# The second matrix of a convolution branch: half of its columns by seven block products instead of eight, in a planned order

## The chip, the core and the metric

The kernel runs on one core of a Trainium2 chip. The engines that matter are TensorE (matrix products; PE in the profile, PEld its weight loads), VectorE (DVE), ScalarE (ACT), and the two queues that start transfers from main memory in this part, SyncE (SP) and GpSimd (POOL). Each engine works through its own list of instructions in order, and waits where an instruction needs something that another engine or a transfer hasn't finished. The metric is the time of one execution on the device, in microseconds (us).

## The reference

One layer of a decoder, 256 tokens and 16 learned ones ahead of them, width D = 2048, all in 32-bit floats:

```python
u = rms_norm(h, g_pre_mix)
proj = u @ w_in          # z_pool 1024 | v_conv 1024 | g_conv 1024 | gate_a 2048 | gate_b 2048
y_a = causal_multiscale_pool(z_pool, w_pool_grp, pool_scale) @ w_pool_out   # 1024 x 2048
a = v_conv * sigmoid(g_conv)
c = depthwise_causal_conv(a, w_dw, 31 taps) + b_dw
y_b = silu(layer_norm(c)) @ w_conv_out                                      # 1024 x 2048
m = sigmoid(gate_a) * y_a + sigmoid(gate_b) * y_b
h = h + rms_norm(m @ w_o)
h = h + rms_norm(square(relu(rms_norm(h) @ w_up)) @ w_down)
```

The change concerns the product with `w_conv_out`, 256 x 1024 times 1024 x 2048, and the work on `c` ahead of it.

## The kernel before

**Products in three terms.** Every factor is split in two parts of a shorter format, a high one (ScalarE casts) and a low one (VectorE subtracts the high part from the original), and a product is the sum of high x high, high x low and low x high. A weight tile is 512 rows by 512 columns (128 partitions x 2048 numbers, 1 MB). It is loaded into one of three rooms named `raw` (SP), cast into one of three `hi` slots and subtracted into one of three `lo` slots; `open_chunk` and `fetch` do that up to two tiles ahead of TensorE. A *block product* is one block of 128 tokens by 512 rows times one weight tile: 4 x 3 = 12 matmuls of 128 x 512 that add up in one bank of the accumulator memory. There are eight banks, six named `acc` and two `misc`.

**Stages.** First the columns of `v_conv` and `g_conv` in tiles of 256 columns (`project`), then `z_pool`, then the sixteen blocks of the two gates (`project_t`, tiles of 5.44 us, 32 of them), the pool's group map, its output matrix (`acc_po`, 8 tiles), the conv's output matrix (`acc_co`, 8 tiles), then W_o (`o_a`, `o_b`, `o_c`), and the two matrices of the feed-forward part. W_o and the feed-forward part already use seven block products for eight (Winograd's form of Strassen's scheme): sums of weight tiles, sums of token blocks, and results added to or subtracted from several outputs. Their order is written out by hand (`STEPS`) and the instructions of each engine are put in order by the class `Plan`: each piece of work has an engine, a cost and the names that it reads and writes; `order` derives from TensorE's sequence when each piece is due, and gives every engine, among the pieces that can start, the one due first. Pieces that no product of the same plan needs have no due time and go in the order in which they were added.

**Work between the products.** Ahead of the plans, vector work is put in a list `pending` with a cost for each item. After each half tile `drain` gives the list a credit, `fill`/2 us, and issues items as long as the credit covers them. What ScalarE must do behind such an item is put in `late` and let go by the next `fetch`, behind that tile's cast. An entry `FETCH` in the list holds the items behind it until `late` is empty.

The 31 taps of the convolution run there: for each of eight tiles of 128 channels (`conv_tile`) one activation and thirty items `c = a[shifted] * tap + c` on VectorE, one after the other. Then come the layer norm's sums. The four steps that end the norm (`ln_items`: normed, with sixteen activations on ScalarE behind it, then swish, low, high) are put at the head of the list when the pool's output matrix begins.

**The conv's output matrix** is plain: for each of four column blocks n two tiles of 512 rows; each tile serves the two blocks of tokens, so two block products per tile, sixteen in all. Behind a column block VectorE multiplies the bank by the gate and adds the pool's part (`evac_conv`, two instructions per block of tokens), and TensorE transposes the result into `m` (`feature_steps`) one column block later. The transposes of the last column block run in W_o's plan behind its first product (`m_last`). Meanwhile GpSimd loads two sums of W_o tiles (`early_sums`): two plain loads, then two that add to what is there.

## Time and profile before

| | us |
|---|---|
| time, median of 3 runs | 1183.82 (1183.77 to 1184.33) |
| the profiled execution, its own time | 1184.32 |
| its span, first to last instruction | 1182.6 |
| TensorE busy | 1172.7 |
| VectorE busy | 1027.6 |
| ScalarE busy | 679.6 |
| pool's output matrix on TensorE | 333.19 to 376.74 |
| conv's output matrix on TensorE | 376.74 to 422.99, four transposes within W_o's first products |

The matmuls overlap in their pipeline, so one lasts longer than the distance to the next; the times of a stage come from the chain of work, where the first number is the start, the second the length, then engine, output and line, and how many instructions. A row of a timeline has the start, the length, the engine, the line, the operation with output and inputs, and in brackets how long the engine was idle before it and what ended that.

### The profile page before, as it was taken

The numbers are of one execution on the slowest core, as the hardware profiler recorded it, in microseconds if no ns is written. First come the engines' busy times: TensorE is split into PE (matmuls) and PEld (weight loads), VectorE is DVE, ScalarE is ACT, GpSimd is POOL, SyncE is SP. The second block draws the span as 40 slices with busy tenths as digits, with TensorE's granted clock in tenths as the row PEclk, the third lists the DMA queues.
The fourth block names the chain that finished last, engine by engine and source line by source line (L and its number), as shares of the span: only waits on it lengthen the run. The fifth ranks groups of instructions, "written<-read, shape, count | busy, mean of one in ns | idle before, by whom it ended". The sixth has DMA issues, their size and how long they took to land.

```text
span 1182.6 us, 15774 instructions
## 1 busy us (share of the span) xinstructions
PE 1172.7 (99%) x6351; PEld 1018.9 (86%) x6351; DVE 1027.6 (87%) x1095; ACT 679.6 (57%) x690; POOL 45.0 (4%) x51
## 2 busy tenths in 40 slices
PE   9999999999999999999999999999999999999997
PEld 9999988888888888898888888888888888888886
DVE  6899978999766799987998988989989989889865
ACT  6533344444584465756566766666656667666642
POOL 1000000000000001000001001000000010010000
PEclk9999999999999999999999999999999999999998
DMA  8655565655647967859869898988998898998861
GB/s 295 214 178 179 182 204 184 196 195 184 208 143 268 265 215 221 290 168 317 248 213 249 228 288 220 269 269 226 281 293 215 267 279 229 282 241 239 303 214 72
DMA packets 177882, 272.91 MB, mean 231 GB/s; under 512 B 4657, under 2 KB 92913, under 8 KB 176912
## 3 DMA queue, kind: packets, MB, share of 16 engines
q1 hardware_dynamic: 160176, 235.88, 59.0%
q0 software_dynamic: 16736, 34.76, 16.2%
q10 hardware_dynamic: 896, 1.25, 0.3%
q8 instruction: 50, 0.82, 0.3%
q14 instruction: 24, 0.20, 0.1%
HBM read 267.68 MB, written 4.19 MB: 230 GB/s over the span
## 4 chain that ended last, share of the span: by engine, by line
PE 99%; DVE 0%; DVEq 0%; issue 0%; ACT 0%; ACTq 0%
PE bank_u L498 18%; PE acc_gate L802 15%; PE bank_a L1787 10%; PE bank_u L504 9%; PE acc_up L1787 8%; PE bank_b L1787 7%; PE o_c L1170 6%; PE acc_z L493 4%; PE acc_co L802 4%; PE acc_po L802 4%; PE acc_v L493 3%; PE acc_g L493 3%; PE acc_vg L493 2%; PE acc_up L498 1%; PE bank_u L1787 1%; PE o_b L1170 1%
## 5 line engine op out<-in xcount | busy, mean ns | idle before, releaser
L498 PE MATMUL bank_u<-m,hi 128*128 128x512 f32 x960 | 329.4, 390 | 0.0
L504 PE MATMUL bank_u<-m,lo 128*128 128x256 f32 x960 | 265.5, 277 | 0.0
L276 ACT CAST hi<-raw 128x2048 fp32r<-128x2048 f32 (+2 forms) x94 | 151.0, 1620 | 188.1 <-PE acc_gate L802 64.0
L498 PEld LDWEIGHTS bank_u<-m,hi 128*128 128x128 f32 x960 | 180.2, 188 | 37.9
L279 DVE TENSOR_TENSOR lo<-raw,hi 128x2048 fp32r<-128x2048 f32 (+2 forms) x94 | 180.0, 1925 | 34.6 <-ACT hi L276 34.1
L1570 DVE TENSOR_TENSOR lo<-raw_m,hi 128x2048 fp32r<-128x2048 f32 x70 | 160.3, 2290 | 31.6 <-ACT hi L1566 31.5
L504 PEld LDWEIGHTS bank_u<-m,lo 128*128 128x128 f32 x960 | 180.3, 188 | 1.4
L1566 ACT CAST hi<-raw_m 128x2048 fp32r<-128x2048 f32 x70 | 133.9, 1912 | 73.7 <-DVE raw_m L1583 21.3
L802 PE MATMUL acc_gate<-hi,u_um 128*128 128x512 f32 x416 | 131.1, 389 | 0.0
L559 DVE SCALAR_TENSOR_TENSOR c<-a,taps,c 128x256 f32<-128x256 f32 x240 | 115.7, 484 | 6.8
L1787 PE MATMUL bank_a<-hi,forms 128*128 128x512 f32 (+1 forms) x288 | 93.5, 386 | 0.0
L802 PEld LDWEIGHTS acc_gate<-hi,u_um 128*128 128x128 f32 x416 | 78.1, 188 | 16.1
L802 PE MATMUL acc_gate<-lo,u_um 128*128 128x512 f32 x208 | 80.9, 389 | 0.0
L1570 DVE TENSOR_TENSOR lo<-raw_a,hi 128x2048 fp32r<-128x2048 f32 x29 | 66.4, 2290 | 10.8 <-ACT hi L1566 10.7
L1566 ACT CAST hi<-raw_a 128x2048 fp32r<-128x2048 f32 x29 | 55.4, 1910 | 35.4 <-PE bank_u L498 13.2
L1566 ACT CAST hi<-raw_c 128x2048 fp32r<-128x2048 f32 x27 | 51.5, 1909 | 27.2 <-PE bank_u L498 12.4
L1570 DVE TENSOR_TENSOR lo<-raw_c,hi 128x2048 fp32r<-128x2048 f32 x27 | 61.8, 2289 | 5.7 <-ACT hi L1566 5.6
L1787 PEld LDWEIGHTS bank_a<-hi,forms 128*128 128x128 f32 x288 | 53.9, 188 | 11.0
L1570 DVE TENSOR_TENSOR fourth_pair<-raw_m,fourth_pair 128x2048 fp32r<-128x2048 f32 x26 | 59.5, 2288 | 4.4 <-ACT fourth_pair L1566 4.4
L1650 ACT COPY half<-bank_u 128x256 f32<-128x256 f32 x60 | 22.2, 370 | 66.0 <-PE bank_u L504 66.0
L1787 PE MATMUL acc_up<-hi,forms 128*128 128x512 f32 x176 | 57.4, 390 | 0.0
L1787 PE MATMUL bank_a<-lo,forms 128*128 128x512 f32 (+1 forms) x144 | 55.6, 386 | 0.0
(419 smaller groups left out, 2265.0 us busy)
## 6 DMA issues: line engine op xcount, KB each, us to landing
raw<-in_w_in_dram SPq DMA_DIRECT2D x52, 1024.0 KB, 5.1
raw_m<-in_w_down_dram SPq DMA_DIRECT2D x38, 1024.0 KB, 7.0
raw_m<-in_w_down_dram POOLq DMA_DIRECT2D x22, 1024.0 KB, 10.6
raw_a<-in_w_up_dram SPq DMA_DIRECT2D x20, 1024.0 KB, 6.4
raw_c<-in_w_up_dram SPq DMA_DIRECT2D x19, 1024.0 KB, 6.9
raw_m<-in_w_up_dram SPq DMA_DIRECT2D x19, 1024.0 KB, 6.9
raw_a<-in_w_down_dram SPq DMA_DIRECT2D x13, 1024.0 KB, 7.3
raw_c<-in_w_down_dram SPq DMA_DIRECT2D x13, 1024.0 KB, 7.3
```

The costliest lines, as they stand in the source:

```text
L276: nc.scalar.copy(hi[:, sl, cs], raw[:, sl, cs])
L279: nc.vector.tensor_sub(lo[:, sl, cs], raw[:, sl, cs], f32(hi[:, sl, cs]))
L493: nc.tensor.matmul(acc, w[:, k[0], cs], act[:, k[1], a, off:], start=first and n == 0, stop=last and n == 2)
L498: nc.tensor.matmul(acc.rearrange("p (a t) -> p a t", a=2)[:, :, ts], hi[:, k[0], cs], act[:, k[1], :, off + ts.start:off + ts.stop], start ...
L504: nc.tensor.matmul(acc[:, :T], lo[:, k[0], cs], act[:, k[1], 0, off:], start=False, stop=stop, skip_group_check=True)
L559: nc.vector.scalar_tensor_tensor(c, conv["a"][:, q, i:i + T], taps[:, q, i:i + 1], c, op0=ALU.mult, op1=ALU.add)
L802: nc.tensor.matmul(acc, act(kk)[:, a_, ts_], w_[:, k, :], start=kk == 0 and n == 0, stop=kk == nk - 1 and n == 2)
L1170: nc.tensor.matmul(acc, form(k, a_), box[w_][:, k, :], start=start and k == 0 and n == 0, stop=stop and k == CK - 1 and n == 2, skip_group ...
L1566: nc.scalar.copy(box["hi"], raw)
L1570: nc.vector.tensor_sub(box["lo"], raw, f32(box["hi"]))
L1650: nc.scalar.copy(box[j], accs[j][:, :T])
L1787: nc.tensor.matmul(acc, forms[h][:, f, k, a_, :], box[w_][:, k, cs], start=start and k == 0 and n == 0, stop=stop and k == KH - 1 and n == ...
```

## The change

The first two column blocks of the conv's output matrix (n = 0 and 1) are computed by seven block products instead of eight, the last two as before. The sequence on TensorE is written out in `ORDER`: units 1 to 7 are the seven products, X20a is column block 2, upper 512 rows, first block of tokens, and so on, f00 is the transposes of column block 0, first tokens. A new plan, `cplan`, orders the stage.

- Products 1, 6, 7 and 4 add up in one bank (`ch`); ScalarE copies what stands there after 1, 6 and 7 (`keep`). 2 has a bank of its own, 5 and 3 share one. VectorE joins copies and banks (`joined`) and applies the gates.
- Three weight tiles are sums of two, two and four tiles. They lie in the room of the gates' input `u` (`conv_wide`, tag `um`), and GpSimd loads them when the gates are done: three plain loads and five that add. Tile 6 is first used as tile 5, and then tile 3 is added to it on VectorE.
- The token blocks' sums (`conv_sums`) and four of their forms (`conv_high`, `conv_low`) are new work of VectorE and ScalarE.
- The two sums of W_o tiles are loaded behind product 3 instead of at the start of the stage.
- The taps of two channel tiles are put into the list alternately (`conv_pair`), the credits rise from 2.4 and 2.5 to 3.0 and 2.9, and the first two steps of the norm move into the gates' stage.
- In the first two column blocks a tile's two parts serve one product; the X tiles still serve two.
- W_o's plan expects VectorE free 3.0 us after its start instead of 2.2.

```diff
-    for w, nk in ((w_pool_out, KP), (w_conv_out, KC)):
-        for n in range(NB):
-            stream += columns(w, 0, nk, n * CW)
+    for n in range(NB):
+        stream += columns(w_pool_out, 0, KP, n * CW)
+
+    def conv_block(kb, n):
+        return columns(w_conv_out, kb * CK, CK, n * CW)[0]
+
+    CONV = ("1", "5", "2", "6", "7", "X20", "3", "4", "X30", "X21", "X31")
+    CONV_LOADS = {"1": (0, 0), "2": (1, 0), "3": (1, 1)}
+    ORDER = "1 5 2 6 7 X20b f00 X20a 3 f11 4 X30a f01 f10 X30b X21a X21b X31a sums f20 X31b f21"
+    UNITS = [u_ for u_ in ORDER.split() if u_[0] not in "fs"]
+    for key in CONV:
+        at_ = CONV_LOADS.get(key) or (key[0] == "X" and (int(key[2]), int(key[1])))
+        stream.append(conv_block(*at_) if at_ and key != "3" else (None, key))
...
+    def open_room(key):
+
+        raw = conv_raw(key)
+        hi, lo = (part_tile(tag, at["parts"]) for tag in ("hi", "lo"))
+        at["parts"] += 1
+
+        more = conv_raw("3") if key == "5" else None
+
+        def f():
+            nc.scalar.copy(hi, raw)
+            nc.vector.tensor_sub(lo, raw, f32(hi))
+            if more is not None:
+                nc.vector.tensor_add(raw, raw, more)
+        opened.append((*(t.rearrange("p (k c) -> p k c", k=CK) for t in (hi, lo)), [f], raw))
+
+    def add_into(room, block_, op=ALU.add):
+        nc.gpsimd.dma_start(room.rearrange("p (k c) -> p k c", k=CK), block_[0],
+                            **({"accum_op": op} if op else {}))
+
+    conv_rooms = {}
+
+    def conv_raw(key):
+
+        if key == "3" and key not in conv_rooms:
+            conv_rooms["3"] = raw = raws.tile([P, CK * CW], F32, tag="raw", name="raw_conv")
+            nc.sync.dma_start(raw.rearrange("p (k c) -> p k c", k=CK), conv_block(1, 1)[0])
+        return conv_rooms[{"5": "6"}.get(key, key)]
...
+    begun_tiles = []
+
+    def conv_pair(q):
+
+        begun_tiles.append(conv_tile(q))
+        if len(begun_tiles) == 2:
+            pending.extend(item for two in zip(*begun_tiles) for item in two)
+            begun_tiles.clear()
...
-                pending.extend(conv_tile(q))
+                conv_pair(q)
...
-        project(u, KD, evac_v, f"v{h}", mm=mm3, width=L, fill=2.5, ahead=1 if h == 1 else 2)
-        project(u, KD, evac_g(h * HALF_CW // P), f"g{h}", mm=mm3, width=L, fill=2.4)
+        project(u, KD, evac_v, f"v{h}", mm=mm3, width=L, fill=3.0, ahead=1 if h == 1 else 2)
+        project(u, KD, evac_g(h * HALF_CW // P), f"g{h}", mm=mm3, width=L, fill=3.0)
...
-                fill=2.5)
+                fill=3.0)
...
+        return [(1.1, f) for f in (normed, swish, low, high)]
+
+    ln_halves = ln_items(0), ln_items(QW)
+    for step in range(2):
+        pending += [FETCH] + [half[step] for half in ln_halves]
...
-            project_t(u_of, KD, evac_gate(b, n), f"gate{b}{n}", fill=2.5)
+            project_t(u_of, KD, evac_gate(b, n), f"gate{b}{n}", fill=2.9)
...
-        a_, b_ = ln_items(0), ln_items(QW)
-        pending[0:0] = [a_[0], b_[0], FETCH, a_[1], b_[1], FETCH, a_[2], b_[2]]
+        a_, b_ = ln_halves
+        for half in ln_halves:
+            late.append(half[3][1])
+        pending[0:0] = [FETCH, a_[2], b_[2],
+                        (2.4, conv_sums), FETCH] + [(0.6, conv_low(key)) for key in "56"]
     pending += [(0, ln_out), (0, ln_act)]
+
+    conv_wide = big.tile([P, 3, CK * CW], F32, tag="um", name="conv_wide")
+
+    sums_ = {"6": ((0, 0), (0, 1)), "7": ((0, 1), (1, 1)), "4": ((0, 0), (0, 1), (1, 1), (1, 0))}
+    for i in range(4):
+        for n, (key, blocks_) in enumerate(sums_.items()):
+            conv_rooms[key] = conv_wide[:, n]
+            if i < len(blocks_):
+                add_into(conv_rooms[key], conv_block(*blocks_[i]), ALU.add if i else None)
+    Sc = {}
+
+    def new_forms(r, **where):
+        Sc[r] = big.tile([P, 2, CK, 2, P], F32R, name=f"conv_forms_{r}", **where)
+    FORM_C = {"5": (0, 0, (1, 0)), "6": (0, 1, (1, 1)), "7": (1, 0, (0, 0)), "3": (1, 1, (0, 1))}
+
+    def conv_a(t, h):
+        return conv["c"][:, h * CK:(h + 1) * CK, t * P:(t + 1) * P]
+
+    def conv_sums():
+        a11, a12, a21, a22 = (conv_a(t, h) for t in range(2) for h in range(2))
+        nc.vector.tensor_sub(a11, a11, a21)
+        nc.vector.tensor_sub(a21, a21, a22)
+        nc.vector.scalar_tensor_tensor(a22, a11, -1.0, a22, op0=ALU.mult, op1=ALU.subtract)
+        nc.vector.tensor_add(a12, a12, a22)
+        new_forms(0, tag="a")
+        late.extend(conv_high(key) for key in "56")
+
+    def conv_high(key):
+        r, f, at_ = FORM_C[key]
+        return lambda: nc.scalar.copy(Sc[r][:, f, :, 0, :], conv_a(*at_))
+
+    def conv_low(key):
+        r, f, at_ = FORM_C[key]
+        return lambda: nc.vector.tensor_sub(Sc[r][:, f, :, 1, :], conv_a(*at_),
+                                            f32(Sc[r][:, f, :, 0, :]))
...
-    for keys, op in ((((0, 0), (0, 1)), {}), (((0, 1), (1, 1)), {"accum_op": ALU.add})):
-        for e, key in enumerate(keys):
-            nc.gpsimd.dma_start(early_sums[:, e].rearrange("p (k c) -> p k c", k=CK),
-                                source_o(key), **op)
...
+    conv_banks = {"ch": acc_tile("acc_co_chain"), "w2": acc_tile("acc_co_2"),
+                  "w3": acc_tile("acc_co_3")}
+    BANK_C = {"1": "ch", "6": "ch", "7": "ch", "4": "ch", "2": "w2", "5": "w3", "3": "w3"}
...
+    def split_c(e, key):
+
+        q, n = slot_c(e), first_c + e
+        box = {}
+
+        def room():
+            return conv_raw(key) if key in ("6", "7", "4", "3") else flats[e]
+        name = {"6": "wide0", "7": "wide1", "4": "wide2", "3": "raw1"}.get(key) or loads_c[e]
+
+        def high():
+            box["hi"] = part_tile("hi", n)
+            nc.scalar.copy(box["hi"], room())
+
+        def low():
+            box["lo"] = part_tile("lo", n)
+            nc.vector.tensor_sub(box["lo"], room(), f32(box["hi"]))
+            conv_parts[e] = tuple(box[h].rearrange("p (k c) -> p k c", k=CK) for h in HALVES)
+        cplan.add("ACT", 1.83, high, reads=(name,), writes=(f"hi{q}",))
+        cplan.add("DVE", 2.22, low, reads=(name, f"hi{q}"), writes=(f"lo{q}",))
...
+    def keep(n, t, bank):
+        cplan.add("ACT", 0.5, lambda: nc.scalar.copy(mt_of(n, t), conv_banks[bank]),
+                  reads=(bank,), writes=(h_of(n, t),))
+
+    def gate_conv(n, t, bank=None):
+        h = h_of(n, t)
+        cplan.add("DVE", 0.62, lambda: nc.vector.tensor_mul(
+            mt_of(n, t), conv_banks[bank] if bank else mt_of(n, t), sg[1][:, t, block(n)]),
+            reads=(bank,) if bank else (h,), writes=(h,))
+        cplan.add("DVE", 0.62, lambda: nc.vector.tensor_add(
+            mt_of(n, t), mt_of(n, t), sg[0][:, t, block(n)]), reads=(h,), writes=(h,))
+
+    def joined(n, t, op, a_, b_, names):
+        cplan.add("DVE", 0.62, lambda: op(mt_of(n, t), a_(), b_()), reads=names,
+                  writes=(h_of(n, t),))
+        gate_conv(n, t)
...
+    loaded = ["2", "X20", "X21", "X30", "X31"]
...
+        q = slot_c(e)
+        cplan.add("PE", 2.72, product, reads=[f"hi{q}", f"lo{q}"] + (
+            ["S" + unit] if unit in FORM_C else []), writes=(bank,))
+        if unit == "1":
+            keep(0, 0, "ch")
+        elif unit == "5":
+            keep(0, 1, "w3")
+        elif unit == "6":
+            keep(1, 0, "ch")
+            cplan.add("ACT", 0.0, place_a, writes=("S5", "S6", "Aroom"))
+        elif unit == "2":
+            joined(0, 0, nc.vector.tensor_add, lambda: conv_banks["w2"], lambda: mt_of(0, 0),
+                   ("w2", h_of(0, 0)))
+        elif unit == "7":
+            keep(1, 1, "ch")
+            joined(1, 1, nc.vector.tensor_sub, lambda: mt_of(0, 1), lambda: mt_of(1, 1),
+                   (h_of(0, 1), h_of(1, 1)))
+        elif unit == "3":
+            joined(1, 0, nc.vector.tensor_sub, lambda: conv_banks["w3"], lambda: mt_of(1, 0),
+                   ("w3", h_of(1, 0)))
+            cplan.add("ACT", 0.0, place_early, writes=("S7", "S3", "early0", "early1"))
+            early_load(0, (0, 0), None)
+            early_load(1, (0, 1), None)
+            early_load(0, (0, 1), ALU.add)
+            early_load(1, (1, 1), ALU.add)
+        elif unit == "4":
+            gate_conv(0, 1, "ch")
+        for item in BEHIND[unit]:
+            if item == "sums":
+                cplan.add("DVE", 2.5, sums_of_m, reads=[f"A{t}{h}" for t in range(2)
+                                                       for h in range(2)], writes=("A",))
+            else:
+                features(int(item[1]), int(item[2]))
+        if X and kb:
+            gate_conv(int(unit[1]), "ab".index(unit[3]), bank)
...
-    plan.add("DVE", 2.2, lambda: None, writes=[f"S{t}{h}" for t in range(2) for h in range(2)]
+    plan.add("DVE", 3.0, lambda: None, writes=[f"S{t}{h}" for t in range(2) for h in range(2)]
```

More of the change, by code (lines that the diff above doesn't have):

```diff
@@ new lines, in hybrid_block, with slot_c, load_c, f @@
+    later = {}
+    first_c = at["parts"] - len(opened)
+    ahead_c = len(opened)
+    conv_parts = {e: opened[e][:2] for e in range(ahead_c)}
+    flats = {}
+    loads_c = {}
+    opened.clear()
+    n_loads = [0]
+    def slot_c(e):
+        return (first_c + e) % 3
+    def load_c(e, src, rows=CK, ahead=False):
+        r = n_loads[0] % 3
+        n_loads[0] += 1
+        loads_c[e] = f"raw{r}"
+        def f():
+            flats[e] = raw = raws.tile([P, CK * CW], F32, tag="raw", name=f"raw_c{e}")
+            nc.sync.dma_start(raw.rearrange("p (k c) -> p k c", k=rows), src)
+        cplan.add("SP", 0.0 if ahead else 3.1, f, writes=(f"raw{r}",), late=0.0 if ahead else 3.0)
@@ new lines, in form_parts, with place_forms, place_mts @@
+    def form_parts(key, late_=False):
+        cplan.add("ACT", 0.53, conv_high(key), reads=("c",), writes=("S" + key,))
+        cplan.add("DVE", 0.62, conv_low(key), reads=("c", "S" + key), writes=("S" + key,))
+    def place_forms():
+        new_forms(1, tag="k8", bufs=2)
+    cplan.add("ACT", 0.0, place_forms, writes=("S7", "S3"))
+    cplan.add("DVE", 1.4, lambda: None, writes=("wide0",))
+    for key in "73":
+        form_parts(key)
+    def place_mts():
+        later["mts"] = big.tile([P, CC // CW * 2, CW], F32, tag="c", name="mts")
@@ L1224, in m_last @@
     def m_last(t):
[L1226 removed]
+        f_pe, f_hi, f_lo, _ = feature_steps(NB - 1, t, mt_of(NB - 1, t))
         plan.add("PE", 0.45, f_pe, writes=(f"mt{t}",))
```

187 lines of the change are left out of this document (139 added, 48 removed).

## The prediction

> **What bounds the kernel now.** I read the page's busy table first, then the chain of work that ended last, then the waits, then the busy time by stage, and last the rows around the changed stage.
>
> ```profile
> span 1182.6 us, 15774 instructions
> PE 1172.7 (99%) x6351; PEld 1018.9 (86%) x6351; DVE 1027.6 (87%) x1095; ACT 679.6 (57%) x690; POOL 45.0 (4%) x51
> PE 99%; DVE 0%; DVEq 0%; issue 0%; ACT 0%; ACTq 0%
> ```
> ```profile
> 34.00:376.70 342.70, 342.70 (x1986) 304.90 (x1986) 302.40 (x406) 158.57 (x138) 0.00 (x0) 1.00 0.58 191
> 376.70:422.80 46.10, 46.10 (x217) 38.40 (x216) 33.52 (x32) 20.58 (x18) 4.16 (x4) 1.00 0.83 251
> 422.80:450.00 27.20, 27.20 (x125) 22.60 (x124) 26.91 (x21) 20.26 (x19) 1.83 (x2) 1.00 0.79 251
> ```
> ```profile
> 333.19 43.55 PE acc_po L802 x192
> 376.74 16.32 PE acc_co L802 x72
> 422.99 2.73 PE o_c L1170 x12
> 425.72 0.87 PE mt L920 x8
> ```
>
> In the stage rows the columns are the stretch, its length, the busy time of PE, PEld, DVE, ACT and POOL, the granted clock, the DMA share and GB/s. TensorE is the chain, and between 34 and 450 us it never waits. So a matmul removed is time removed, and a wait added to TensorE is time added. The second row is the changed stage: VectorE works 33.52 of 46.10 us, so 12.6 us idle there are the cover that the change may spend. In the stage behind it VectorE has 0.3 us left of 27.2. DMA is already at 0.83.
>
> **The change, part by part.** Times are counted from the first conv product (376.74 in this trace).
>
> *Products.* One 128x512 matmul takes 43.55/192 = 0.2268 us, one block product of twelve 2.72 us. Sixteen become fifteen, the eight transposes stay: -2.72 us. Nothing else leaves TensorE's program, so this is the largest gain there can be.
>
> *The running bank.* Products 1, 6, 7 and 4 add into one bank, and ScalarE copies its state out behind 1, 6 and 7. In the order 7 stands directly behind 6, so TensorE waits for the copy behind 6. The price is in these rows of the next stage:
>
> ```profile
> 434.38 0.39 PE L1170 MATMUL o_a<-hi,m 128*128 128x512 f32 x1
> 434.85 1.92 ACT L1118 CAST hi<-early_sums 128x2048 fp32r<-128x2048 f32 x1 [0.81 <-PE o_a L1170]
> 482.86 0.58 ACT L1209 COPY og<-o_b 128x512 f32<-128x512 f32 x1
> 483.49 0.19 PEld L1170 LDWEIGHTS o_b<-hi,forms_o 128*128 128x128 f32 x1 [0.19 <-ACT og L1209]
> 483.57 0.42 PE L1170 MATMUL o_b<-hi,forms_o 128*128 128x512 f32 x1
> ```
>
> The last matmul lasts 0.39 us, ScalarE starts 0.08 us behind its end (434.77 to 434.85), copies for 0.58, and the matmul starts 0.13 us behind the copy (483.44 to 483.57). That is 1.18 us from start to start where 0.23 is usual: +0.95. It is 2.86 if ScalarE has just begun a cast of 1.91 us. I take 0.95: the split of X20 ends near 10.1 us and product 6 at 10.9, and nothing else is ready for ScalarE between.
>
> *Splits.* A split tile now feeds one product of 2.72 us, where it fed two:
>
> ```profile
> 376.77 1.91 ACT L276 CAST hi<-raw 128x2048 fp32r<-128x2048 f32 x1 [2.01 <-PE acc_po L802]
> 378.72 2.29 DVE L279 TENSOR_TENSOR lo<-raw,hi 128x2048 fp32r<-128x2048 f32 x1 [1.25 <-ACT hi L276]
> 401.35 0.68 DVE L938 TENSOR_TENSOR mts<-acc_co,sg 128x512 f32<-128x512 f32 x1
> 402.06 0.69 DVE L939 TENSOR_TENSOR mts<-mts,sg 128x512 f32<-128x512 f32 x1
> 402.67 0.69 DVE L938 TENSOR_TENSOR mts<-acc_co,sg 128x512 f32<-128x512 f32 x1
> 424.31 0.69 DVE L939 TENSOR_TENSOR mts<-mts,sg 128x512 f32<-128x512 f32 x1
> 424.98 2.29 DVE L1123 TENSOR_TENSOR lo<-raw_o,hi 128x2048 fp32r<-128x2048 f32 x1
> ```
>
> From the slot's release to the finished low part are 4.3 us. With three slots the window is two products, 5.44 us: 1.1 us to spare for 2, 6, 7 and X20, more later. They fit as long as VectorE stands free, so they cost nothing in front. ScalarE has 25 us idle (second stage row) and gets three casts, four copies and two forms, 9 us: nothing but the bank's wait.
>
> VectorE's account of the stage: three more low parts, 6.6 us (at 2.2, the next instruction starting before the end); the addition that makes tile 6, 2.2; three joins, 2.0; two low forms, 1.3; together 12.1. The stage is 1.8 us shorter. 12.6 - 12.1 - 1.8 = -1.3: no idle is left, though about 2 us of it can't be used, since low parts wait for casts as in the second row above. Today VectorE ends its conv work 2.2 us behind the stage (424.98 against 422.8); then it is 2.2 + 1.3 + about 0.6 = 4.1. The first to need that end are the transposes of the last column block (425.72), one product and one transpose behind the stage, 3.2 us: +0.9. Bounds: 0 when the gates go ahead of other work, 2.4 when the 2 us of idle come on top whole. This late VectorE also eats the next stage's margin:
>
> ```profile
> 434.07 2.29 DVE L1123 TENSOR_TENSOR lo<-raw_o,hi 128x2048 fp32r<-128x2048 f32 x1
> 434.77 5.44 PE o_c L1170 x24
> ```
>
> The low part of P3 ends at 436.36, its product starts at 437.49. TensorE being 0.9 late itself, that margin of 1.1 covers the remaining lag of 1.0: nothing.
>
> *Taps in turn.* A tap reads what the tap before wrote:
>
> ```profile
> 53.67 3.09 DVE L559 SCALAR_TENSOR_TENSOR c<-a,taps,c 128x256 f32<-128x256 f32 x6
> 82.28 1.52 DVE L559 SCALAR_TENSOR_TENSOR c<-a,taps,c 128x256 f32<-128x256 f32 x3
> 83.71 0.43 DVE L573 TENSOR_TENSOR g<-acc_g,rb 128x272 f32<-128x272 f32 x1
> ```
>
> Six take 3.09, so they start every 0.52 us (less the last one's 0.48); an instruction that doesn't depend on the third tap starts 83.71 - 82.28 - 2 x 0.52 = 0.39 behind it. Two tiles in turn should therefore go at 0.39. A gate tile with a fill of 2.9 gets 2.9/0.39 = 7.4 taps: 2.9 + 2.2 = 5.1 us against 5.44 of TensorE. No cost, no gain, but the taps end some seven gate tiles earlier. That room takes the normalisation's four steps. The Trainium skill (VectorE: DVE Perf Modes, The DRAIN you can't avoid) says that the next operation starts only when the pipe is empty and that chaining doesn't avoid it; by that the turns gain nothing, which is the last rival. The two spacings here speak against it for this pair.
>
> *Normalisation in the gate stage.* Its sixteen activations run on ScalarE in one block:
>
> ```profile
> 340.51 0.59 ACT L868 ACTIVATE sq<-c,vecs 128x256 f32<-128x256 f32 x1
> 349.54 1.90 ACT L276 CAST hi<-raw 128x2048 fp32r<-128x2048 f32 x1
> 351.47 2.29 DVE L279 TENSOR_TENSOR lo<-raw,hi 128x2048 fp32r<-128x2048 f32 x1 [0.58 <-ACT hi L276]
> ```
>
> From 340.5 the block holds the next cast until 349.54; its low part ends at 353.76, and TensorE wants it at 333.19 + 4 x 5.44 = 354.95. Gate tiles have the same length, so the same 1.2 us cover it. By the credits of the work list (2.9 a gate tile: pool items 11.7, the 34 of taps left, then the statistics, whose breaks stretch them to nine tiles) the block is let go in tile 27 and the gates' two sigmoids in 28: nothing; together they would cost 0.1.
>
> *Merged tiles.* Three plain and five adding loads of 1 MB go on POOL's queue when the gates end, 327.4; today's four stand behind them and move to product 3.
>
> ```profile
> 377.04 1.57 POOL L906 DMA_DIRECT2D early_sums<-in_w_o_dram  x2 [371.21 <-PE acc_po L802]
> 384.98 1.30 POOL L906 DMA_DIRECT2D early_sums<-in_w_o_dram  x1 [6.37 <-DMA early_sums<-in_w_o_dram]
> 388.50 1.28 POOL L906 DMA_DIRECT2D early_sums<-in_w_o_dram  x1 [2.22 <-DMA early_sums<-in_w_o_dram]
> DMA to landing us min/median/max: 7.4/11.8/18.0
> ```
>
> Two plain loads land in 11.5 us (377.0 to 388.5); the last add lands 18.0 behind its issue, 406.5, so two adds take 18 us, 9 each. Estimate: three plain loads until 343, three adds until 370, two more in sequence, with 2 us of restart each, until 392. Tile 6 is wanted at 371 (pool tile 6 ended), 7 at 382 (product 5 ended), 4 at 391 and at the latest 396, 4.3 us ahead of its product: nothing. Tile loads on SP slow down beside the adds (up to 14.9 us below; the cast it kept waiting lost 0.74). In the pool stage a load is issued 11.9 us ahead of the earliest and 18 ahead of the latest cast (16.3 - 4.4, + 6.5): nothing. X30's load starts at 390, when X20's low part frees a room; its cast must start by 398.7: nothing, at worst 390 + 14.9 - 398.7 = 6.
>
> ```profile
> DMA to landing us min/median/max: 5.0/5.2/14.9
> 399.84 1.92 ACT L276 CAST hi<-raw 128x2048 fp32r<-128x2048 f32 x1 [0.74 <-DMA raw<-in_w_conv_out_dram]
> raw_o<-in_w_o_dram SPq DMA_DIRECT2D x10, 1024.0 KB, 5.6
> ```
>
> The four loads of the W_o sums now start at 400, behind product 3: the first sum lands near 421, P5's cast must start by 429: nothing. P3's tile goes to the room of the last gate rows: issued at 424.7, its cast is due at 431.3, 6.6 us against a median of 5.6: nothing, at worst 1.
>
> *Sum.* -2.72 + 0.95 + 0.9 = -0.87. The profiled execution is 1184.32 us (span 1182.6 and 1.7 around it), so 1183.45 for it; it lies 0.5 above the median of the runs, 1183.82, from which the same sum gives 1182.95.
>
> **The rivals.** *No wait at the bank* (faster). TensorE waits for nothing here, and if the copy and the late gates are hidden too, -2.72 stands: 1181.1. For it: the copy of R6's bank cost nothing in the rows above. Against: a whole product lay between R6 and R7, and none between 6 and 7.
>
> *The merged tile 4 lands late* (slower). Its four loads run one behind the other. ScalarE takes casts in order, so a cast that waits for tile 4 holds those of X30 and X21. Beyond 396 us each microsecond costs one. At 13 us an add instead of 9 (the slowest landing above is 18) it lands at 343 + 65 + 4 = 412: +16, 1199. From 10.4 us an add (399.2) the kernel is slower than before by 0.2%. For it: DMA share 0.83 already with half of the adds. Against: only 0.58 before 376. If TensorE then stood still for over 3.4 us, the Trainium skill (TensorE: Matmul & The Clock Gate, HAM oscillation) lets its clock fall to half; no run here shows that, the granted clock being 1.00 in every row quoted.
>
> *Taps don't get shorter in turn* (slower).
>
> ```profile
> 47.43 11.84 PE acc_g L493 x96
> 106.63 46.18 PE acc_z L493 x384
> 152.81 146.89 PE acc_gate L802 x648
> ```
>
> At 0.52 a gate tile (146.89/27 = 5.44) needs 7.4 x 0.52 + 2.2 = 6.1 us of VectorE: 0.6 over, in 13 tiles with taps 8. The twelve tiles of 11.84/2 = 5.92 and the eight of 46.18/8 = 5.77 before them need 7.7 x 0.52 + 2.2 and 0.4 of products' ends, 6.6: 15 over. Less some 8 that the tiles split ahead hold: +15, 1198. For it: every pair of taps in the trace is spaced so. Against: the 0.39 to an instruction that doesn't depend.
>
> **How the numbers follow.** Measurements of this kernel can tell about 0.2% from no change, 2.4 us. The forecast, with its small stalls in 1181.9 to 1184.5, 0.70; no wait 0.09; tile 4 late 0.15; taps 0.06. The forecast lies within 0.2%: same 0.70, faster 0.09, slower 0.21. The time is the forecast's, 1182.9. The range goes from the rival without a wait, 1181.1, to the forecast with both upper bounds (1182.95 + 1.9 + 1.5), 1186.3.
>
> **What would show it.** Right: 180 conv matmuls; a gap of 0.9 to 1.0 us on TensorE between products 6 and 7 with a ScalarE copy in it; VectorE without idle time from there on and about 4 us late at the stage's end; a wait of TensorE before the last transposes; taps every 0.39 us. Wrong: no gap behind 6; a cast that waits for a DMA by several us; TensorE waits in the gates or in the pool stage, which I cost at nothing.

## The result, and the profile after

The changed kernel takes 1195.05 us (median; 1193.89 to 1196.07), the kernel before 1184.07 beside it: the ratio is 1.0091, with an interval from 1.0078 to 1.0103. It is 11 us slower, where 1182.9 was forecast and 1186.3 was the upper end of the range.

The page of the changed kernel first, its totals and its chain of work:

```profile
span 1193.3 us, 15793 instructions
PE 1174.1 (98%) x6339; PEld 1018.6 (85%) x6339; DVE 1027.4 (86%) x1110; ACT 688.9 (58%) x701; POOL 53.9 (5%) x59
PE 91%; DMA 5%; DVE 2%; ACT 1%; issue 0%; DVEq 0%; ACTq 0%; SPq 0%
```

TensorE was 99% of the chain; now 5% of it, some 60 us, are DMA. The chain in order of time (start, length, what) says which transfers:

```profile
332.10 15.68 DMA raw<-in_w_pool_out_dram
352.15 16.61 DMA raw<-in_w_pool_out_dram
373.12 9.19 DMA raw_c<-in_w_conv_out_dram
412.33 14.06 DMA raw_c<-in_w_o_dram
435.81 7.59 PE o_c L1476 x24
```

None of them is a load of the merged tiles. They are ordinary tile loads on SP: two for the pool stage, the one of conv tile 2, and the second tile of W_o. The waits of TensorE (what waited, for what, us in total, times, longest):

```profile
PE mt L1006 <- DVE mts L1120: 4.1, 1, 4.1
PE acc_co L1222 <- DVE lo L1073: 1.8, 1, 1.8
PE acc_po L881 <- DVE lo L293: 1.7, 1, 1.7
PE mt L1006 <- DVE pairs L1120: 1.3, 1, 1.3
PE acc_co_chain L1222 <- ACT pairs L1112: 0.7, 1, 0.7
```

Only the last was in the sum as such, and 0.9 of the two `mt` rows. Behind each of the others stands a late load. Where the time went is read best from the starts of the first matmul of each stage, here as lengths from one to the next; the third column is a run from the next section, in which the adding loads are left out:

| stretch of TensorE's program | before | changed | without the adds |
|---|---|---|---|
| pool stage, first product to first conv product | 43.54 | 45.61 | 43.55 |
| conv stage, to P2's first matmul | 46.26 | 46.67 | 44.53 |
| P2 and the last transposes, to X02 | 3.52 | 9.79 | 4.21 |
| X02, to P1 | 5.54 | 7.77 | 5.55 |
| sum | 98.86 | 109.84 | 97.84 |

The sum grows by 10.98 us, and the span by 10.7: the loss lies between 333 and 443 us, and nothing ahead of it or behind it matters. X02 is 24 matmuls, as before, yet takes 2.2 us longer: its clock is down. The busy time by stretch (stretch, length, PE, PEld, DVE, ACT, POOL, granted clock, DMA share, GB/s) shows that, and the DMA:

```profile
333.40:366.50 33.10, 33.06 (x147) 27.04 (x145) 20.17 (x22) 12.92 (x11) 3.85 (x3) 1.00 1.08 299
429.00:435.40 6.40, 1.30 (x8) 1.12 (x9) 5.51 (x7) 2.16 (x2) 0.00 (x0) 0.84 0.57 126
435.40:440.30 4.90, 4.90 (x14) 3.86 (x14) 4.76 (x3) 4.90 (x8) 0.00 (x0) 0.51 0.98 369
```

In the pool stage the DMA engines are full for 33 us (share 1.08, where it was 0.59 before; as the queue rows below show, the shares of the two queues add up to more than 1). The tile loads that SP issued between 325 and 376 us, first in the kernel before, then in the changed one, from issue to landing:

```profile
DMA to landing us min/median/max: 5.0/5.1/5.4
```
```profile
DMA to landing us min/median/max: 11.1/16.1/19.7
```

At the conv stage's end the second W_o tile is 14.1 us on its way (6.1 in the kernel before), and these rows show what its cast holds up (start, length, instruction, in brackets the idle time before it and its cause):

```profile
426.49 1.91 ACT L1069 CAST hi<-raw_c 128x2048 fp32r<-128x2048 f32 x1 [8.26 <-DMA raw_c<-in_w_o_dram]
428.44 2.29 DVE L1073 TENSOR_TENSOR lo<-raw_c,hi 128x2048 fp32r<-128x2048 f32 x1 [5.13 <-ACT hi L1069]
432.80 0.63 PE L1006 MATMUL mt<-ident,mts 128*128 128x128 f32 x4 [4.11 <-DVE mts L1120]
434.73 1.08 PE L1006 MATMUL mt<-ident,pairs 128*128 128x128 f32 x4 [1.30 <-DVE pairs L1120]
```

ScalarE waits for the tile, VectorE's low part waits for ScalarE, the last four gates stand behind that low part, and the transposes need the gates. VectorE is idle for 5.13 us in the stage where it has none to spare.

### The profile page after: what moved, and what is told of

Same layout as the page of the kernel before. It is cut to its first block, busy times and chain, and to the rows that moved or that the text cites. A ratio compares the mean times of both kernels' runs of the same rounds, so it can differ in the third digit from the quotient of the medians.

```text
span 1193.3 us, 15793 instructions
## 1 busy us (share of the span) xinstructions
PE 1174.1 (98%) x6339; PEld 1018.6 (85%) x6339; DVE 1027.4 (86%) x1110; ACT 688.9 (58%) x701; POOL 53.9 (5%) x59
## 4 chain that ended last, share of the span: by engine, by line
PE 91%; DMA 5%; DVE 2%; ACT 1%; issue 0%; DVEq 0%; ACTq 0%; SPq 0%
PE bank_u L540 18%; PE acc_gate L881 15%; PE bank_a L2093 10%; PE bank_u L546 9%; PE acc_up L2093 8%; PE bank_b L2093 7%; PE o_c L1476 5%; PE acc_z L535 4%; PE acc_v L535 3%; PE acc_g L535 3%; DMA raw<-in_w_pool_out_dram 3%; PE acc_vg L535 2%; PE acc_up L540 1%; DMA raw_c<-in_w_o_dram 1%; PE bank_u L2093 1%; DMA raw_c<-in_w_conv_out_dram 1%
## 5 line engine op out<-in xcount | busy, mean ns | idle before, releaser
L290 ACT CAST hi<-raw 128x2048 fp32r<-128x2048 f32 (+2 forms) x85 | 133.8, 1588 | 178.1 <-PE acc_gate L881 37.6
L293 DVE TENSOR_TENSOR lo<-raw,hi 128x2048 fp32r<-128x2048 f32 (+2 forms) x85 | 159.3, 1886 | 52.9 <-ACT hi L290 52.6
L601 DVE SCALAR_TENSOR_TENSOR c<-a,taps,c 128x256 f32<-128x256 f32 x240 | 98.4, 475 | 0.1
L881 PEld LDWEIGHTS acc_gate<-hi,u_um 128*128 128x128 f32 x416 | 78.1, 188 | 16.1
L1876 DVE TENSOR_TENSOR lo<-raw_a,hi 128x2048 fp32r<-128x2048 f32 x29 | 66.3, 2287 | 10.8 <-ACT hi L1872 10.7
```

What stands on the lines that cost most here:

```text
L290: nc.scalar.copy(hi[:, sl, cs], raw[:, sl, cs])
L293: nc.vector.tensor_sub(lo[:, sl, cs], raw[:, sl, cs], f32(hi[:, sl, cs]))
L601: nc.vector.scalar_tensor_tensor(c, conv["a"][:, q, i:i + T], taps[:, q, i:i + 1], c, op0=ALU.mult, op1=ALU.add)
L881: nc.tensor.matmul(acc, act(kk)[:, a_, ts_], w_[:, k, :], start=kk == 0 and n == 0, stop=kk == nk - 1 and n == 2)
L1876: nc.vector.tensor_sub(box["lo"], raw, f32(box["hi"]))
```

## The experiments

Theory: the adding loads on GpSimd's queue take so much of the DMA engines that ordinary tile loads beside them come late; everything else costs what the prediction said. Rivals: VectorE is out of time in the conv stage, whatever the loads do; or the early part of the change costs something.

**One part alone, and the adds left out.** `early_part` is the kernel before with only the taps of two tiles in turn, the larger fills and the normalisation in the gate stage. The other three are the changed kernel without adding loads:

```
-            if i < len(blocks_):
+            if i < len(blocks_) and not i:
...
-            early_load(0, (0, 1), ALU.add)
-            early_load(1, (1, 1), ALU.add)
```

The first edit is `no_adds_pool`, the second `no_adds_wo`, both together `no_adds`.

> The kernel before with only the early part of the change: taps of two tiles in turn, the larger fills, the normalisation in the gate stage; conv stage, its products and all loads as before. Theory: no change, 1184 (between 1183 and 1185), since TensorE shows no wait before 366 us in the changed kernel. Rival (the early part costs time that the trace hides elsewhere): 1186 or more.

> The changed kernel without the five adding loads of the merged weight tiles; the three plain loads stay, so tiles 6, 7 and 4 hold one block each and half of the first two output column blocks is wrong. Theory (the adding loads slow the tile loads on SP): the casts of the pool stage stop waiting for DMA, TensorE no longer waits at the end of the pool stage (1.7 us) nor at product 2 (1.8 us), the first conv product starts near 376.8 instead of 379.0: about 4 us less, 1191. The wait at the conv stage's end (4.1 + 1.3) stays. Rival (VectorE's and ScalarE's own work in the pool and conv stages is too much): no change, 1195.

> The changed kernel without the two adding loads of the W_o sums (plain loads stay; those two tiles of W_o hold one block each, so part of the output is wrong). Theory (the adds delay the load of the second W_o tile, its cast holds ScalarE's queue and the last gates behind it): the cast's wait of 8.3 us goes, of TensorE's wait of 5.4 us before the last transposes about 1 is left, and the 2.3 us of matmuls at half rate behind it go: about 7 less, 1188. Rival (VectorE is simply out of time in the conv stage): the wait stays at 4 us or more, 1194 or above.

> Both sets of adding loads left out (part of the output wrong, as in the two kernels with one set left out). Theory: the two gains add up to about 11 us, 1184, and what is left is the prediction's own sum: 2.7 less of products, 0.9 more at the running bank, about 1 more before the last transposes, 1183 to 1184. Rival (VectorE is out of time): 1189 or above.

| kernel | us, median (lowest to highest) | ratio to before, interval |
|---|---|---|
| early_part | 1184.15 (1183.33 to 1184.87) | 0.9999, 0.9989 to 1.0008 |
| no_adds_pool | 1190.73 (1190.66 to 1190.89) | 1.0053, 1.0036 to 1.0070 |
| no_adds_wo | 1185.86 (1184.85 to 1189.32) | 1.0019, 1.0009 to 1.0028 |
| no_adds | 1183.18 (1183.02 to 1183.43) | 0.9990, 0.9981 to 1.0000 |

The early part costs nothing. Without the adds of the merged tiles 4.3 us are gone, without those of the W_o sums 9.2, without both 11.9, which is all of the loss; left without its adds the change takes 1183.2, near the forecast of 1182.9. TensorE's waits in no_adds:

```profile
PE acc_co_chain L1222 <- ACT pairs L1112: 0.7, 1, 0.7
PE mt L1006 <- DVE pairs L1120: 0.4, 1, 0.4
```

These are the bank's wait and the wait before the last transposes, the two that the sum had. So the rival of VectorE's time falls as the main cause, at least for the 11 us. In no_adds_wo 1.4 us more than the stall and the slow clock went: its waits in the pool stage and at product 2 were 0.7 and 0.8, where the changed kernel has 1.7 and 1.8. Nothing was changed there. The same holds for `wo_split_last` and `adds_behind_wo` below, whose program is that of the changed kernel up to product 2: the pool stage took 45.61 us in the changed kernel and 44.51, 44.13 and 44.37 in these three, and the wait at product 2 was 1.8, 0.8, 1.0 and 1.7. So what these late loads cost differs by some 2 us from one profiled execution to another, which covers the 1.4, and also that the two gains by themselves add up to 13.5 and not to 11.9.

**Bytes, or adding?** The seven adds became plain loads of the same blocks to the same places:

```
-                add_into(conv_rooms[key], conv_block(*blocks_[i]), ALU.add if i else None)
+                add_into(conv_rooms[key], conv_block(*blocks_[i]), None)
-            early_load(0, (0, 1), ALU.add)
-            early_load(1, (1, 1), ALU.add)
+            early_load(0, (0, 1), None)
+            early_load(1, (1, 1), None)
```

> The changed kernel with all seven adding loads (five for the merged tiles, two for the W_o sums) turned into plain loads of the same blocks into the same places, one behind the other as before: as many bytes on the same queue, nothing added, so those tiles hold one block each and part of the output is wrong. Rival (the bytes do it): the waits stay, 1193 or more. Theory (an adding load holds the 16 DMA engines longer than a plain one; in the changed kernel a stretch with adds moved 260 to 270 GB/s at full share, one with plain loads 400): nearly all of the 11.9 us that leaving out the adds saved comes back, 1183 to 1186.

It takes 1188.2 us (1187.86 to 1189.45), ratio 1.0034 (1.0021 to 1.0047). 6.9 of the 11.9 us come back, where the theory expected nearly all: with equal bytes the adding makes somewhat more than half of the loss and the bytes themselves the rest. In the pool stage all of it came back (TensorE has no wait there); at the stage's end a shorter stall stays:

```profile
PE mt L1006 <- DVE mts L1120: 2.2, 1, 2.2
PE mt L1006 <- DVE pairs L1120: 1.3, 1, 1.3
```

The price of an add can be read from the list of DMA queues (q0 is GpSimd's, q1 SP's: packets, MB, time of the packets as a share of 16 engines). First the changed kernel from 340 to 366 us, then the plain loads in the same stretch:

```profile
DMA packets 3513, 7.01 MB, mean 270 GB/s; under 512 B 111, under 2 KB 111, under 8 KB 3512
q0 software_dynamic: 1598, 3.20, 65.7%
q1 hardware_dynamic: 1914, 3.80, 43.3%
```
```profile
DMA packets 4014, 10.04 MB, mean 386 GB/s; under 512 B 161, under 2 KB 161, under 8 KB 4013
q1 hardware_dynamic: 2907, 5.76, 59.9%
q0 software_dynamic: 1106, 4.26, 41.1%
```

An added MB takes the engines for 26 x 0.657 / 3.20 = 5.3 us, a plain one for 26 x 0.411 / 4.26 = 2.5. Shares that sum to 109% overlap, so here is a second estimate that doesn't use them: the plain stretch moved a MB in 26 / 10.04 = 2.6 us, at which SP's 3.80 MB in the first stretch need 9.8, and the 16.2 us left make 5.0 for each of the 3.20 added ones. Either way an add costs about two plain loads. The trace of before had this row too, in the stretch from 389 to 406 us, where an add of the W_o sums runs:

```profile
q0 software_dynamic: 998, 1.98, 63.8%
q1 hardware_dynamic: 1306, 2.61, 43.9%
```

17 x 0.638 / 1.98 = 5.5 us for an added MB, 2.9 for a loaded one. With these the account, as an estimate, would have been: from 326 to 385 us eight tile loads on SP (23), three plain ones (7.5) and five adds (27.5), 58 us of transfers in 59. The loads that SP issued in that stretch landed 8.7 to 19.7 us behind their issue, none in 5.

**What the late W_o tile holds up.** `wo_split_last` lets its split follow the last gates and features (the names it now also has to wait for), with all loads as they were:

```
-        while split_done < len(CONV) + 2 and used.get(split_done - 3, -1) < u_ and split_done <= e + 3:
+        while split_done < len(CONV) + 1 and used.get(split_done - 3, -1) < u_ and split_done <= e + 3:
...
-        split_c(split_done, "w_o")
+        split_c(split_done, "w_o", (h_of(3, 0), h_of(3, 1), "m21l"))
```

> The changed kernel with one cast and one low part moved: the split of the second W_o tile stands behind the last two gates and their features in ScalarE's and VectorE's order instead of ahead of them; all loads and all results as they were. Theory (the tile's late load costs by what its cast holds up): the gates run by 427.5, TensorE's wait before the last transposes (5.4) goes, a wait of about 2 for the tile itself appears behind them, too short for the clock to fall, so the matmuls at half rate (2.3) go too: 1188 to 1189. Rival (the lateness of the tile costs by itself, wherever its cast stands): 1193 or more.

It takes 1192.69 us (1191.86 to 1198.22), ratio 1.0086 (1.0062 to 1.0111), near the rival's 1193. The waits before the last transposes went, and others came:

```profile
PE o_a L1476 <- DVE m L1015: 4.6, 1, 4.6
PE acc_co L1222 <- DVE lo L1073: 1.0, 1, 1.0
PE o_c L1476 <- DVE lo L1073: 0.9, 1, 0.9
```

The 4.6 us stand one product later: the cast of the next W_o tile, late as well (ScalarE waited 5.4 us for it), stands ahead of the features of the last block. The theory was right on the mechanism, a cast that waits holds what stands behind it, and wrong on the gain, because the next load was late too. The 2.4 us that it lies below the changed kernel are about what the pool stage and product 2 happened to lose less in the profiled execution (1.5 and 0.8), so the move itself is not shown to have gained anything.

`adds_behind_wo` lets GpSimd copy one column of that tile ahead of the two adds, so they start when it has landed:

```
-            early_load(0, (0, 1), ALU.add)
-            early_load(1, (1, 1), ALU.add)
...
+        nc.gpsimd.tensor_copy(t, flats[W_O[1]][:, :1])
...
+    early_load(0, (0, 1), ALU.add)
+    early_load(1, (1, 1), ALU.add)
```

> The changed kernel with the two adds of the W_o sums held back: GpSimd copies one column of the second W_o tile ahead of them, so they start when that tile has landed; all results as they were. Theory: the tile lands some 6 us behind its issue, as without the adds, the wait before the last transposes falls to about 0.5: 1186 to 1187. Rival (the sums, some 8 us later, are now late themselves): the cast of the first sum waits for DMA, TensorE waits in the W_o stage, 1190 or more.

1189.99 us (1189.36 to 1194.03), ratio 1.0055 (1.0039 to 1.0072): the rival came true. The wait before the transposes is 0.4, as without the adds, and now the sums are late:

```profile
PE o_c L1482 <- DVE forms_o L1474: 2.5, 1, 2.5
ACT hi L1430 <- DMA early_sums<-in_w_o_dram: 2.1, 1, 2.1
```

**Fewer loads.** Merged tile 4 is tile 6 and one block more, so `lean` adds that block into tile 6's room once 6 is split. Five loads do for eight:

```
-    sums_ = {"6": ((0, 0), (0, 1)), "7": ((0, 1), (1, 1)), "4": ((0, 0), (0, 1), (1, 1), (1, 0))}
+    sums_ = {"6": ((0, 0), (0, 1)), "7": ((0, 1), (1, 1))}
+    conv_rooms["4"] = conv_wide[:, 0]
...
+            if key == "6":
+                cplan.add("POOL", 5.6, lambda: add_into(conv_rooms["4"], conv_block(1, 0)),
+                          reads=("wide0",), writes=("wide0",), late=4.0)
```

> The changed kernel with merged tile 4 made from merged tile 6: once 6 is split, one adding load brings the missing fourth block into its place; tile 4's own plain load and three adds go (five loads on GpSimd's queue for eight, all results as they were). Theory: two plain loads and two adds are done near 352, the casts of the pool stage wait little, product 2 does not wait, about 4 us less: 1191. Rival (the late add, near 385, comes too late for tile 4 or delays X30 and X21): tile 4's cast waits for DMA and the gain is gone, 1194 or more.

1191.23 us (1190.55 to 1191.6), ratio 1.0058 (1.0043 to 1.0073), as the theory said, and half a microsecond from no_adds_pool. TensorE has no wait in the pool stage or at product 2, and the stall at the stage's end is the whole loss:

```profile
PE mt L1007 <- DVE mts L1121: 4.6, 1, 4.6
PE mt L1007 <- DVE pairs L1121: 0.8, 1, 0.8
```

**Looking for an order that pays.** From `lean` on, `sums_early` gives the forms of products 7 and 3 the places of those of 5 and 6, so that the room of the W_o sums is free at the pool stage's end and their loads start near 377, and f00 stands behind product 3; `x30_first` also loads X30's tile ahead of X21's; `x30_features_first` also puts X21's cast behind the features of the first two tiles. The two named "apart" also put half of X20 between products 6 and 7.

```
-    FORM_C = {"5": (0, 0, (1, 0)), "6": (0, 1, (1, 1)), "7": (1, 0, (0, 0)), "3": (1, 1, (0, 1))}
+    FORM_C = {"5": (0, 0, (1, 0)), "6": (0, 1, (1, 1)), "7": (0, 0, (0, 0)), "3": (0, 1, (0, 1))}
...
+    for e in range(2):
+        add_into(early_sums[:, e], (source_o((0, e)),), None)
...
-    ORDER = "1 5 2 6 7 X20b X20a 3 f00 f11 4 X30a f01 f10 X30b X21a X21b X31a sums f20 X31b f21"
+    ORDER = "1 5 2 6 X20b 7 X20a 3 f00 4 f11 X30a f01 f10 X30b X21a X21b X31a sums f20 X31b f21"
...
-    loaded = ["2", "X20", "X21", "X30", "X31"]
+    loaded = ["2", "X20", "X30", "X21", "X31"]
```

The first two edits are `sums_early`, the third is "apart", the last `x30_first`.

> The kernel with merged tile 4 made from tile 6 (three loads fewer), and in addition the W_o sums back where they were before: the forms of products 7 and 3 take the places of those of 5 and 6, so the room of the sums is free at the pool stage's end and their two plain loads start near 377, tile 4's add near 384, the two adds of the sums behind it; f00's transposes stand behind product 3. All results as they were. Theory (the waits come from adds beside urgent loads; the sums' loads leave the stretch from 400 to 425): no cast waits for DMA by more than 1 us near the stage's end, only the bank's wait of 0.9 and about 0.5 before the last transposes are left: 1183, not distinguishable from before or 0.1% faster. Rival (the adds now disturb tile 4 or the loads of X30 and X21 near 385 to 400): TensorE waits there, 1187 or more.

> The same as sums_early, and product 7 is no longer directly behind product 6 on the running bank: one half of X20 stands between them (order 1 5 2 6 X20b 7 X20a 3 f00 4 f11). Theory (the bank's wait of 0.9 us is the copy behind product 6 and nothing else): 0.9 less than sums_early, about 1182, faster than the kernel before by 0.2%. Rival (the splits, in another order now, wait in its place): the same as sums_early or slower.

> sums_early with X30's tile loaded before X21's (X30 is used first; X21's load stood ahead of it): X30's load is issued near 382, before the three adds, X21's and X31's behind it. All results as they were. Theory (only a load that is urgent while adds run costs time): X30's cast does not wait, X21 and X31 have 12 us or more each until their casts are due, so TensorE waits only at the bank (0.9) and about 0.5 before the last transposes: 1183. Rival (the adds hold back any tile load whatever its slack): X21's or X31's cast waits for DMA by several us, 1187 or more.

> sums_early_apart with the same change of the load order. Theory: no cast waits for DMA, no wait at the running bank: 0.9 below x30_first, about 1182. Rival (ScalarE's and VectorE's order with X20 ahead of 7 makes new waits): not below x30_first.

> x30_first with one ScalarE cast moved: X21's cast stands behind the feature casts of the first two tiles (f00, f11) instead of ahead of them. All results as they were. Theory (ScalarE's order holds the features): TensorE's waits of 2.2 and 0.6 near 408 go, and the slow matmuls behind them: 1183 to 1184. Rival (what is left in x30_first is X31's late load): the wait only moves, 1187 or more.

| kernel | us, median (lowest to highest) | ratio to before, interval |
|---|---|---|
| sums_early | 1190.09 (1189.13 to 1191.07) | 1.0050, 1.0037 to 1.0063 |
| sums_early_apart | 1194.19 (1193.79 to 1194.83) | 1.0086, 1.0072 to 1.0099 |
| x30_first | 1187.92 (1187.03 to 1188.37) | 1.0031, 1.0020 to 1.0042 |
| x30_first_apart | 1191.27 (1190.56 to 1191.92) | 1.0061, 1.0049 to 1.0074 |
| x30_features_first | 1188.94 (1186.31 to 1189.75) | 1.0036, 1.0024 to 1.0049 |

None reached the 1182 to 1184 that the theory expected. In sums_early the three adds now run from 384 to 405, and X30's cast waits for its tile:

```profile
404.05 1.90 ACT L1072 CAST hi<-raw_c 128x2048 fp32r<-128x2048 f32 x1 [7.33 <-DMA raw_c<-in_w_conv_out_dram]
```

With X30 loaded first that wait is gone and X31's cast waits instead (3.2 us). TensorE waits 2.2 us for a gate that stands in VectorE's queue behind the first features, which stand behind X21's cast in ScalarE's. With those features ahead of the cast the 2.2 go too (of two waits there one of 0.6 is left), and waits of 1.2, 1.1 and 1.3 us come up at later transposes, so the time is no better than in x30_first. No order got rid of the waits; each moved them to another place. In both "apart" kernels TensorE no longer waits for the copy behind product 6, and both are slower than their pair, since other waits come (6.6 us for X30's late tile in the first; 5.7 in the second for features behind a cast that waits 5.1 for its late tile). Whether some order of the loads reaches 1183 with every add in it stays open; the five tried don't, and even a kernel with no wait but the bank's would by the sum be only 1.8 us faster than the kernel before.

**The bank's wait by itself.** In no_adds, the copy behind product 6 reads product 5's finished bank:

```
-            keep(1, 0, "ch")
+            keep(1, 0, "w3")
```

> no_adds, and the copy behind product 6 reads the finished bank of product 5 instead of the running bank, so product 7 has nothing to wait for (one more tile of the output is wrong, beside those of no_adds; the work is the same). Theory (the bank's wait is on the chain): 0.9 less than no_adds, 1182.2 to 1182.4. Rival (the 0.9 are taken up later anyway, by VectorE's late end): as no_adds, 1183.2.

1182.49 us (1181.56 to 1182.87), ratio 0.9985 (0.9976 to 0.9994): 0.7 less than no_adds by the medians, with intervals that overlap. TensorE's only wait behind 34 us is then the one before the last transposes, 0.6 where it was 0.4, so what the bank's wait cost (0.83 by the rows below) comes back but for 0.2.

## Why the prediction was wrong, point by point

- **Products, -2.72, and the running bank, +0.95: right.** Without the adds the conv stage goes from 46.26 to 44.53, so by -1.73, against -1.77. In the changed kernel itself the bank's gap is as forecast, the copy between the last matmul of 6 and the first of 7:

```profile
391.79 0.39 PE L1222 MATMUL acc_co_chain<-hi,conv_forms 128*128 128x512 f32 x1
392.21 0.58 ACT L1112 COPY pairs<-acc_co_chain 128x512 f32<-128x512 f32 x1 [0.80 <-PE acc_co_chain L1222]
392.85 0.50 PE L1222 MATMUL acc_co_chain<-hi,conv_forms 128*128 128x512 f32 x1 [0.68 <-ACT pairs L1112]
```

  1.06 us from start to start where 0.23 is usual: 0.83 for 0.95.

- **VectorE's late end, +0.9: right in kind, 0.7 in size.** In no_adds the stretch of the last transposes grows from 3.52 to 4.21. The last gate ends 3.7 us behind the stage's end (421.70 there), where 4.1 was forecast:

```profile
424.69 0.69 DVE L1120 TENSOR_TENSOR pairs<-pairs,sg 128x512 f32<-128x512 f32 x1
```

- **Splits fit: right.** No product in no_adds waits for a low part.

- **Taps in turn: right.** Four taps take 1.66 us, so one every (1.66 - 0.48) / 3 = 0.39, and all of them wait 0.1 us in sum. The rival in which the turns gain nothing is out:

```profile
59.90 1.66 DVE L601 SCALAR_TENSOR_TENSOR c<-a,taps,c 128x256 f32<-128x256 f32 x4
```
```profile
L601 DVE SCALAR_TENSOR_TENSOR c<-a,taps,c 128x256 f32<-128x256 f32 x240 | 98.4, 475 | 0.1
```

- **Normalisation in the gate stage, nothing: right.** early_part takes 1184.15 for 1184.24 beside it.

- **Merged tiles, nothing: wrong, the first step that failed.** The step asked when the merged tiles land, and there it was right: the three adds side by side were done at 367.3 us where it had 370, the last of all at 390.3 where it had 392, and tile 4's cast did not wait for DMA, so the rival of the late tile 4 did not happen. What it took for covered was the other side: "In the pool stage a load is issued 11.9 us ahead of the earliest and 18 ahead of the latest cast: nothing", with 14.9 as the longest landing. The loads took 11.1 to 19.7, with a median of 16.1, so five casts waited 3.0 to 6.2 us for DMA. One room shows why the slack runs out: its loads start at 332.10 and 352.15 in the chain above, so a round of load, cast and low part takes 20 us, where TensorE uses up the tiles of three rooms in 16.3. The cost was 2.1 us in the pool stage and about 2 at product 2. The term that was mis-sized is the landing of SP's loads beside the adds; behind it stands the DMA time of an add, 5.3 to 5.5 us a MB, which the queue rows of before gave and which was never worked out.

- **W_o sums behind product 3, nothing: wrong, the second step and the larger.** It asked whether the sums are late for P5, and not whom their loads delay. The two tiles of W_o that the stage itself splits were in no term of the sum; the second took 14.1 us instead of 6.1 and its cast held ScalarE for 8.3. That cost 6.3 us up to X02, of which 0.9 were in the sum. The late loads that the prediction did name, at worst 6 us for X30 and 1 for P3, were left out of its range, whose upper end adds only the bounds of the bank and of VectorE.

- **A clock that falls: named in the rival of tile 4 alone.** It came from the stall at the stage's end instead, 2.2 us. The clock was 0.51 from 435.4 to 440.3 us, and matmuls that start every 0.23 us started every 0.43. That the clock falls to half after a standstill of over 3.4 us is what the Trainium skill (TensorE: Matmul & The Clock Gate, HAM oscillation) states. The fall here, behind 4.1 and 1.3 us of standstill, agrees with that, but another run doesn't: in adds_behind_wo a single one of 2.5 us was enough (last section), and there the measurement decides.

Of the signs named, the gap behind 6, the taps and the wait before the transposes came as "right", and "a cast that waits for a DMA by several us" and a wait of TensorE in the pool stage as "wrong".

## What to carry to other kernels

A transfer has two costs: when it lands, and what it does to the transfers beside it. Work out the second from the queue rows, MB against share of time, for each kind of transfer, and sum the DMA time of a whole stretch with every load in it before calling a load hidden. Then look at what stands behind a cast in an in-order queue: a load that is 8 us late there stops engines that need nothing of it.

## What the runs showed of the hardware

- An adding load takes the DMA engines 5.3 to 5.5 us a MB by the shares of the queues (5.0 by the second estimate), a plain load from the same queue 2.5. With adds on their way the engines moved 270 GB/s at a share of 1.09, with plain loads in their place 386 at 1.01 (340 to 366 us).

- The clock does not need a standstill of 3.4 us. In adds_behind_wo TensorE works without a gap from 428.4 to 437.1 at a clock of 1.00, waits 2.49 us, and the matmuls behind the wait start every 0.42 us instead of 0.23 until about 443:

```profile
439.58 1.22 PE L1482 MATMUL o_c<-hi,forms_o 128*128 128x512 f32 x2 [2.49 <-DVE forms_o L1474]
```
```profile
439.50:444.00 4.50, 4.42 (x13) 3.52 (x14) 4.50 (x4) 2.50 (x3) 0.00 (x0) 0.64 1.05 386
```

  A single wait of 1.8 us, at product 2 of the changed kernel, left the clock at 1.00.

- Transposes between the waits don't prevent the fall. In x30_features_first the last large matmul ends at 426.31 and the next starts at 430.03, with two groups of four transposes in between and no wait over 1.3 us, and the next ones run slow:

```profile
427.37 0.63 PE L1009 MATMUL mt<-ident,mts 128*128 128x128 f32 x4 [1.06 <-DVE mts L1117]
429.29 1.08 PE L1009 MATMUL mt<-ident,pairs 128*128 128x128 f32 x4 [1.30 <-DVE pairs L1117]
```
```profile
429.60:434.00 4.40, 4.40 (x17) 3.65 (x16) 4.40 (x3) 2.66 (x5) 0.00 (x0) 0.70 0.95 344
```

  So eight transposes in 3.7 us did not count as work enough; that they count for something isn't shown. In the changed kernel the four transposes right behind 4.11 us of standstill still took 0.63 us, as at full clock, and those behind the next wait 1.08. How long a standstill it takes is therefore not one number in these runs: 2.49 us were enough in one, and 4.11 had not yet done it in another.
